# A third buffer for raw weight blocks, in place of most of the scratch for dynamic DMAs

## The chip, the cores and the metric

The kernel runs on one core of one Trainium2 chip. The metric is the time of one execution on the device in microseconds (us), lower is better. Before and after compute the same outputs from the same inputs, all in fp32; matrix products are done in three passes of a rounded type (below). Engines are named as the profile names them: PE (matmul), PEld (PE's weight load), DVE (vector), ACT (scalar), POOL (GpSimd), SP (the queue from which all DMAs here are issued).

## What is computed

Two blocks, one after the other, on 512 tokens of 1024 features (16 learned tokens are put ahead in the first). The first has a state-space mixer with 16 heads (SSD), a second mixer of 64 small diagonal recurrences (S5), and an MLP; the second is two layers of convolution, neighbourhood attention, a gated merge and a convolutional FFN, with a context stream of 256 tokens beside the main one. Cut to the part in which the change reorders most:

```python
proj = n @ w_in[layer]                 # z, xbc, dt and u, from the normed tokens
xbc = jax.nn.silu(_causal_depthwise_conv(proj[..., o_xbc:o_dt], conv_w[layer], conv_b[layer]))
y_ssd = _ssd_mixer(xbc, dt_raw, z, ...)
y_s5 = _s5_mixer(u, ...)               # recurrence over time in 64 groups, then:
#   y = gelu(y);  v = y @ w_glu + b_glu;  y = v[:, :D_S5] * sigmoid(v[:, D_S5:])
h = h + concatenate([y_ssd, y_s5]) @ w_out[layer]
h = h + square(relu(rmsnorm(h) @ w_up[layer])) @ w_down[layer]
return second_block(first_block(...), c_2, ctx_2, ...)
```

## The kernel before

**Weights.** All large weights stream from HBM once, in blocks of 128 partitions x 1024 fp32 (512 KB, 4 KB of each partition; some are narrower). The helper `W` (lines 222 to 242) fetches one: a DMA on SP into a tile `raw`, of which there are RAW buffers; ACT rounds it to the type fp32r (`whi`, line 239); DVE subtracts, so that `wlo` = raw - whi (line 241). Of `whi` and `wlo` there are HL = 3 buffers each. A raw buffer is free when its line 241 has read it.

```python
with self.tc.high_priority(offset=self.AHEAD):
    raw = self.wp.tile([P, 1024], F32, tag="raw", name=f"raw{i}", bufs=self.RAW)[:, :cols]
    nc.sync.dma_start(raw, src[:, part * cols:(part + 1) * cols])
with self.tc.high_priority(offset=self.SPLIT):
    ...
    hi = part("hi")
    nc.scalar.copy(hi, raw)
    lo = part("lo")
    nc.vector.tensor_sub(lo, raw, hi.bitcast(F32))
```

**Products.** `gemm` calls `mm3` (lines 247 to 249) for each block of 128 features: whi x high part, whi x low part, wlo x high part of the activations, three matmuls into one PSUM tile. A block of 1024 x 128 with 528 tokens is 48 matmuls of 264 columns.

**Order.** A tile framework schedules the program: it lets each engine's instructions run in an order that it chooses at build time from its own estimate of durations and from priorities, and puts the waits between them. AHEAD = 100 and SPLIT = 70 let a weight's DMA and its two roundings go ahead of work that was written before them. At run time each engine then works strictly in that order.

**The first block's mixers** (`build`, about 50 to 306 us). The letters of ORDER interleave two sorts of work. One is gemms on independent weights: `xbc_proj` (twelve, tiles `xbc`), `z_proj` (`z0` to `z3`, two weights each) and `dt_proj` (`dt`). The other is eight rounds of S5: `s5_prepare` m makes three tables (X transposed on PE at line 815, tile XT, and copied to P; Y; K from a product Kp at line 836, written into M by eight small DMAs at line 849), `s5_scan` m runs the recurrence. A scan is a chain over three engines: PE line 873 (S), ACT 875 (copy), PE 877 (Sp), DVE 878 and 879, twice; then DVE 880 (add), ACT 882 and POOL 883, DVE 885 (the scan proper), PE 888 (Zp), DVE 889 to 891, PE lines 894 and 896 (sixteen pairs of small matmuls in all, tile y5m), ACT 899, and a DMA to DRAM (900). Tables of round m+1 are made beside the scan of round m. When all eight are done, `s5_result` loads them back (DMA 906), ACT applies gelu and rounds (lines 908 and 912, tiles yt and y50h), and `glu` starts its gemms (tiles glug and glua), which need all of it. In a row of order, a tile's first digit is the round or the number of the gemm: XT7_0 is round 7, first half; z3 and dt are the last two gemms of the in-projection.

**The context stream.** Beside the main one the second block has gemms on 256 tokens (`ctx_mix`, tiles cxg, cxb, cxo, up to 1055 us), in which a weight is used for half as long.

**Memory.** The program is built with the default scratch for dynamic DMAs, 16 KB of each partition.

Of the kernel before, what the change touches and what calls it, by code (L numbers as in the profile page):

```python
# [190 lines left out]
class Builder:  # L191
    AHEAD = 100
    CONV = (600, 300)
    ADALOW, CXCONV = 0, 0
    RAW = 2
    HL = 3
    TABLES = 5
    ADA1 = 12
# [23 lines left out]
    def W(self, name, *idx, cols=1024, part=0, tags=None):  # L222
# [8 lines left out]
# [3 lines that stand above are left out]
# [1492 lines left out]


# [11 lines left out]
```

## Time and profile before

| | us |
|---|---|
| median of 3 runs | 2740.7 (2732.67 to 2740.95) |
| the profiled execution | 2738.33 |
| its span, first to last instruction | 2736.6 |
| busy PE / DVE / ACT / POOL in it | 2675.2 / 2041.1 / 1165.5 / 6.0 |
| mean granted TensorE clock | 0.995 of full |

Times inside the kernel are microseconds from the start of the span of the profiled execution. A busy PE is not one at its peak: matmuls overlap in the pipeline, so that a matmul of 264 columns has a duration of 0.28 us while the next starts 0.12 us after it. The distance between starts is therefore what a matmul costs.

### The profile page before, as it was taken

The numbers are of one execution on the slowest core, as the hardware profiler recorded it, in microseconds if no ns is written. First come the engines' busy times: TensorE is split into PE (matmuls) and PEld (weight loads), VectorE is DVE, ScalarE is ACT, GpSimd is POOL, SyncE is SP. The second block draws the span as 40 slices with busy tenths as digits, with TensorE's granted clock in tenths as the row PEclk, the third lists the DMA queues.
The fourth block names the chain that finished last, engine by engine and source line by source line (L and its number), as shares of the span: only waits on it lengthen the run. The fifth ranks groups of instructions, "written<-read, shape, count | busy, mean of one in ns | idle before, by whom it ended". The sixth has DMA issues, their size and how long they took to land.

```text
span 2736.6 us, 39800 instructions
## 1 busy us (share of the span) xinstructions
PE 2675.2 (98%) x15107; PEld 2269.9 (83%) x15107; DVE 2041.1 (75%) x3986; ACT 1165.5 (43%) x1961; POOL 6.0 (0%) x52
## 2 busy tenths in 40 slices
PE   8999899999999999999999999999999999999998
PEld 8898678788887898777788888888887777988887
DVE  7987678999885675898669888644769976655556
ACT  4443664433543553445454232322553454534333
POOL 0000000000000000000000000000000000000000
PEclk9999999999999999999999999999999999999999
DMA  6222435566332345322324446211342223232322
GB/s 210 72 82 76 120 124 169 165 205 196 124 108 96 121 148 181 97 89 85 106 85 148 149 153 217 93 61 63 106 145 92 89 66 96 92 97 87 109 93 77
DMA packets 157390, 321.02 MB, mean 117 GB/s; under 512 B 39760, under 2 KB 60688, under 8 KB 157200
## 3 DMA queue, kind: packets, MB, share of 16 engines
q1 hardware_dynamic: 157200, 318.49, 36.9%
q8 instruction: 119, 1.95, 0.3%
q14 instruction: 71, 0.58, 0.1%
HBM read 306.53 MB, written 9.54 MB: 115 GB/s over the span
## 4 chain that ended last, share of the span: by engine, by line
PE 78%; DVE 12%; DMA 4%; ACT 3%; issue 2%; SPq 0%; DVEq 0%; ACTq 0%; POOL 0%
PE lat1fu L247 3%; PE lat1fu L249 3%; PE lat1fu L248 3%; DVE wlo L241 3%; PE lat0fu L248 3%; PE lat0fu L247 3%; PE lat0fu L249 3%; PE dn L247 2%; PE dn L249 2%; PE dn L248 2%; PE up L248 2%; PE up L247 2%; PE up L249 2%; PE lat1d L248 1%; PE lat1d L247 1%
## 5 line engine op out<-in xcount | busy, mean ns | idle before, releaser
L239 ACT CAST whi<-raw 128x1024 fp32r<-128x1024 f32 (+3 forms) x486 | 456.7, 940 | 854.5 <-PE ctx0d L248 118.5
L241 DVE TENSOR_TENSOR wlo<-raw,whi 128x1024 fp32r<-128x1024 f32 (+3 forms) x486 | 526.7, 1084 | 196.2 <-ACT whi L239 190.3
L248 PE MATMUL ctx0fu<-ctx0fx,whi 128*128 128x256 f32 x352 | 99.7, 283 | 0.0
L249 PE MATMUL ctx0fu<-ctx0fx,wlo 128*128 128x256 f32 x352 | 99.6, 283 | 0.0
L247 PE MATMUL ctx0fu<-ctx0fx,whi 128*128 128x256 f32 x352 | 99.5, 283 | 0.0
L1137 DVE SCALAR_TENSOR_TENSOR lat0cv<-lat0u,vect,lat0cv 128x512 f32<-128x512 f32 x120 | 85.7, 746 | 0.5
L1137 DVE SCALAR_TENSOR_TENSOR lat1cv<-lat1u,vect,lat1cv 128x512 f32<-128x512 f32 x120 | 85.7, 744 | 0.5
L1468 DVE SCALAR_TENSOR_TENSOR lat0fc<-lat0fu,vect,lat0fc 128x511 f32<-128x511 f32 x44 | 32.9, 748 | 63.5 <-ACT lat0fc L1467 63.5
L248 PEld LDWEIGHTS ctx0fu<-ctx0fx,whi 128*128 128x128 f32 x352 | 67.4, 191 | 1.6
L247 PEld LDWEIGHTS ctx0fu<-ctx0fx,whi 128*128 128x128 f32 x352 | 67.4, 191 | 1.6
L249 PEld LDWEIGHTS ctx0fu<-ctx0fx,wlo 128*128 128x128 f32 x352 | 67.4, 191 | 0.0
L1467 ACT ACTIVATE lat0fc<-lat0fu,vect 128x512 f32<-128x512 f32 x44 | 34.3, 778 | 74.5 <-PE lat0fu L249 74.5
L1508 DVE SCALAR_TENSOR_TENSOR hT<-lat1d,mod1lat,hT 128x512 f32<-128x512 f32 (+1 forms) x40 | 25.5, 643 | 48.2 <-PE lat1d L249 48.0
L1137 DVE SCALAR_TENSOR_TENSOR cxcv<-cxu,vect,cxcv 128x256 f32<-128x256 f32 x120 | 52.6, 480 | 0.8
L249 PE MATMUL ctx0d<-ctx0fh,wlo 128*128 128x256 f32 x176 | 50.5, 288 | 0.5 <-DVE wlo L241 0.5
L248 PE MATMUL ctx0d<-ctx0fh,whi 128*128 128x256 f32 x176 | 50.4, 287 | 0.0
L247 PE MATMUL ctx0d<-ctx0fh,whi 128*128 128x256 f32 x176 | 50.0, 285 | 0.2 <-ACT whi L239 0.2
L988 DVE TENSOR_TENSOR hT<-hT,dn 128x512 f32<-128x512 f32 x40 | 27.4, 684 | 28.7 <-PE dn L249 28.7
L981 DVE SCALAR_TENSOR_TENSOR r<-up,rsbm 128x512 f32<-128x512 f32 x32 | 22.1, 690 | 31.7 <-PE up L249 31.7
L1508 DVE SCALAR_TENSOR_TENSOR hT<-lat0d,mod0lat,hT 128x512 f32<-128x512 f32 x32 | 23.9, 748 | 20.9 <-PE lat0d L249 20.9
L249 PE MATMUL cxg<-cxn1x,wlo 128*128 128x256 f32 x128 | 36.3, 284 | 0.4 <-DVE wlo L241 0.4
L247 PE MATMUL cxg<-cxn1x,whi 128*128 128x256 f32 x128 | 36.3, 284 | 0.0
(3104 smaller groups left out, 8944.2 us busy)
## 6 DMA issues: line engine op xcount, KB each, us to landing
raw<-in_p_in SPq DMA_DIRECT2D x100, 512.0 KB, 3.5
aw<-in_ada SPq DMA_DIRECT2D x192, 256.0 KB, 3.1
raw<-in_p_up SPq DMA_DIRECT2D x88, 512.0 KB, 3.5
raw<-in_p_dn SPq DMA_DIRECT2D x48, 384.0 KB, 3.0
raw<-in_w_up SPq DMA_DIRECT2D x32, 512.0 KB, 3.6
raw<-in_p_cn SPq DMA_DIRECT2D x48, 256.0 KB, 2.6
raw<-in_w_down SPq DMA_DIRECT2D x24, 384.0 KB, 3.0
raw<-in_p_out SPq DMA_DIRECT2D x18, 512.0 KB, 3.6
```

Source lines behind the costliest of these rows:

```text
L239: nc.scalar.copy(hi, raw)
L241: nc.vector.tensor_sub(lo, raw, hi.bitcast(F32))
L247: mm(ps, w[0], x[0], start=first, stop=False)
L248: mm(ps, w[0], x[1], start=False, stop=False)
L249: mm(ps, w[1], x[0], start=False, stop=last)
L981: V.scalar_tensor_tensor(r, ps, 0.0, rsb, op0=ALU.max, op1=ALU.mult)
L988: V.tensor_add(h[f], h[f], ps)
L1137: V.scalar_tensor_tensor(ac, u[:, k:k + n], self.vec(f"cdw{l}", 4 * k + i), ac, op0=ALU.mult, op1=ALU.add)
L1467: A.activation(u, ps[:, :n], AF.Identity, scale=wv(1), bias=self.vec(f"fdwb{l}", t))
L1468: V.scalar_tensor_tensor(u[:, 1:], ps[:, :n - 1], wv(0), u[:, 1:], op0=ALU.mult, op1=ALU.add)
L1508: V.scalar_tensor_tensor(x, ps, self.mod[l, kind][:, 40 + f:41 + f], x, op0=ALU.mult, op1=ALU.add)
```

## The change

RAW goes from 2 to 3, so 4 KB more of each partition hold raw blocks, and the scratch for dynamic DMAs is cut from 16 KB to 4 KB of each partition. No instruction is added or removed. The schedule is made anew with the third buffer.

```diff
-    RAW = 2
+    RAW = 3
...
-    nc = bacc.Bacc("TRN2", target_bir_lowering=False, num_devices=1)
+    nc = bacc.Bacc("TRN2", target_bir_lowering=False, num_devices=1,
+                   dynamic_dma_scratch_size=4096)
```

Of the 14,370 matmul instructions on PE, some 1,250 stand at another place in the order; 1,059 of these lie between 100 and 283 us of the trace before. Three places follow.

On PE, the start of the tables of the last S5 round (XT7) and of the scan of the one before (S6), as it stood before; dt is a gemm of the in-projection:

```order
L247 MATMUL dt_1_2973<-xg0h_103,whi26_2968 16x264
L248 MATMUL dt_1_2973<-xg0l_104,whi26_2968 16x264
L815 MATMUL XT7_0_2273<-cst_78,X7_2263 128x128 x4
L815 MATMUL XT7_1_2279<-cst_78,X7_2263 128x128 x4
L836 MATMUL Kp7_0_2295<-Y7_2285,bc7_2261 16x128 x4
L836 MATMUL Kp7_1_2301<-Y7_2285,bc7_2261 16x128 x4
L873 MATMUL S6_0_2331<-hT5_86,P6_2017 128x66 x4
L249 MATMUL dt_0_2972<-xg0h_103,wlo26_2970 16x264
L249 MATMUL dt_1_2973<-xg0h_103,wlo26_2970 16x264
L247 MATMUL dt_0_2972<-xg1h_107,whi26_2968 16x264
```

The same place in the changed kernel; z3 is the last gemm of the in-projection, and the two rows shown of it are its last two:

```order
L248 MATMUL z3_1_3065<-wlo28_3124,xg7h_131 128x256
L249 MATMUL z3_1_3065<-whi28_3122,xg7l_132 128x256
L815 MATMUL XT7_0_2273<-cst_78,X7_2263 128x128 x4
L815 MATMUL XT7_1_2279<-cst_78,X7_2263 128x128 x4
L836 MATMUL Kp7_0_2295<-Y7_2285,bc7_2261 16x128 x4
L836 MATMUL Kp7_1_2301<-Y7_2285,bc7_2261 16x128 x4
L873 MATMUL S6_0_2331<-hT5_86,P6_2017 128x66 x4
L877 MATMUL Sp6_0_2337<-S6_2330,cst_78 128x264
L873 MATMUL S6_1_2341<-hT5_86,P6_2017 128x66 x4
L877 MATMUL Sp6_1_2347<-S6_2330,cst_78 128x264
L888 MATMUL Zp6_0_2355<-S6_2330,cst_78 128x264
L888 MATMUL Zp6_1_2359<-S6_2330,cst_78 128x264
```

Before, 140 matmuls of gemms stood between XT7 and the last row of the S5 scans (44 of dt, 96 of z3); now all 140 stand ahead of XT7 and none behind it.

On PE, the first half of the scan of round 1, before:

```order
L873 MATMUL S1_0_1272<-hT2_83,P1_958 128x66 x4
L249 MATMUL xbc1_0_1644<-xg0h_103,wlo13_1642 128x264
L249 MATMUL xbc1_1_1645<-xg0h_103,wlo13_1642 128x264
L247 MATMUL xbc1_0_1644<-xg1h_107,whi13_1640 128x264
L248 MATMUL xbc1_0_1644<-xg1l_108,whi13_1640 128x264
L249 MATMUL xbc1_0_1644<-xg1h_107,wlo13_1642 128x264
L247 MATMUL xbc1_1_1645<-xg1h_107,whi13_1640 128x264
L248 MATMUL xbc1_1_1645<-xg1l_108,whi13_1640 128x264
L249 MATMUL xbc1_1_1645<-xg1h_107,wlo13_1642 128x264
L247 MATMUL xbc1_0_1644<-xg2h_111,whi13_1640 128x264
L248 MATMUL xbc1_0_1644<-xg2l_112,whi13_1640 128x264
L877 MATMUL Sp1_0_1278<-S1_1271,cst_78 128x264
```

and now:

```order
L873 MATMUL S1_0_1272<-hT2_83,P1_958 128x66 x4
L247 MATMUL xbc2_0_2135<-xg0h_103,whi16_2131 128x264
L248 MATMUL xbc2_0_2135<-xg0l_104,whi16_2131 128x264
L877 MATMUL Sp1_0_1278<-S1_1271,cst_78 128x264
L873 MATMUL S1_1_1282<-hT2_83,P1_958 128x66 x4
L247 MATMUL xbc2_1_2136<-xg0h_103,whi16_2131 128x264
L248 MATMUL xbc2_1_2136<-xg0l_104,whi16_2131 128x264
L877 MATMUL Sp1_1_1288<-S1_1271,cst_78 128x264
```

Ten gemm matmuls stood between S and Sp there, now two; in the other rounds up to the sixth they are between 2 and 18.

On DVE, the middle of the scan of round 6, before (wlo28 is the last weight of z3):

```order
L880 TENSOR_TENSOR t6_2320<-t6_2320,f6_2319 128x528
L565 SCALAR_TENSOR_TENSOR xbcT7_2960<-xr7_2956,vect_79,xbcT7_2960 128x528
L241 TENSOR_TENSOR wlo28_3124<-raw28_3120,whi28_3122 128x1024
L885 SCALAR_TENSOR_TENSOR S6_2330<-f6_2319,t6_2320 128x528
L890 TENSOR_TENSOR t6_2320<-S6_2330,cs6_2322 128x264 x2
```

and now:

```order
L880 TENSOR_TENSOR t6_2320<-t6_2320,f6_2319 128x528
L885 SCALAR_TENSOR_TENSOR S6_2330<-f6_2319,t6_2320 128x528
L890 TENSOR_TENSOR t6_2320<-S6_2330,cs6_2322 128x264 x2
L889 TENSOR_TENSOR f6_2319<-Zp6_0_2355,sn6_2321 128x264
L889 TENSOR_TENSOR f6_2319<-Zp6_1_2359,sn6_2321 128x264
```

The work of the gemms on DVE (the convolution of line 565, the residue of line 241) has moved ahead of the chain of the scan.

## Rows read from the trace of the kernel before

**Rows 1.** The page, part 1: busy time of each engine, share, instructions.

```profile
PE 2675.2 (98%) x15107; PEld 2269.9 (83%) x15107; DVE 2041.1 (75%) x3986; ACT 1165.5 (43%) x1961; POOL 6.0 (0%) x52
```

**Rows 2.** One stretch: from:to length, busy us by engine, clock, DMA share, GB/s.

```profile
246.27:282.60 36.33, 35.01 (x280) 31.72 (x278) 24.61 (x43) 16.04 (x28) 0.23 (x2) 1.00 0.31 96
```

**Rows 3.** Waits of PE from 88 to 246 us: total us, times, longest.

```profile
PE Zp L888 <- DVE S L885: 2.6, 6, 0.7
PE xbc L247 <- ACT whi L239: 2.4, 2, 1.3
PE xbc L249 <- DVE wlo L241: 1.4, 1, 1.4
```

**Rows 4.** PE in order of time, end of S5: start, us, instruction, idle before.

```profile
246.27 1.04 PE L815 MATMUL XT<-cst,X 128*128 128x128 f32 x8
...
252.09 0.61 PE L877 MATMUL Sp<-S,cst 128*128 128x264 f32 x2
...
259.61 1.13 PE L888 MATMUL Zp<-S,cst 128*128 128x264 f32 x4 [0.48 <-DVE S L885]
...
262.40 0.33 PE L896 MATMUL y<-t,Y 128*128 128x64 f32 x2
...
269.64 0.61 PE L877 MATMUL Sp<-S,cst 128*128 128x264 f32 x2
...
279.06 0.43 PE L896 MATMUL y<-t,Y 128*128 128x64 f32 x2 [0.33 <-DVE t L891]
...
282.24 0.39 PE L896 MATMUL y<-t,Y 128*128 128x64 f32 x2
...
290.59 0.80 PE L247 MATMUL glug<-y50h,whi 128*128 128x512 f32 x1 [7.61 <-ACT y50h L912]
```

**Rows 5.** DVE in order of time, the same stretch.

```profile
255.78 0.70 DVE L880 TENSOR_TENSOR t<-t,f 128x528 f32<-128x528 f32 x1
256.40 0.76 DVE L565 SCALAR_TENSOR_TENSOR xbcT<-xr,vect,xbcT 128x528 f32<-128x528 f32 x1
257.08 1.22 DVE L241 TENSOR_TENSOR wlo<-raw,whi 128x1024 fp32r<-128x1024 f32 x1
258.21 1.25 DVE L885 TENSOR_TENSOR_SCAN S<-f,t 128x528 f32<-128x528 f32 x1
...
275.70 1.20 DVE L241 TENSOR_TENSOR wlo<-raw,whi 128x1024 fp32r<-128x1024 f32 x1
```

**Rows 6.** ACT in order of time, the same stretch.

```profile
251.39 0.35 ACT L875 COPY S<-S 128x264 f32<-128x264 f32 x1
...
267.99 0.37 ACT L875 COPY S<-S 128x264 f32<-128x264 f32 x1
```

**Rows 7.** PE in order of time: two neighbours of a gemm.

```profile
124.01 0.28 PE L249 MATMUL z<-whi,xg0l 128*128 128x256 f32 x1
124.13 0.28 PE L247 MATMUL z<-whi,xg1h 128*128 128x256 f32 x1
```

**Rows 8.** PE in order of time: XT transposes, four each, at three places.

```profile
68.53 0.66 PE L815 MATMUL XT<-cst,X 128*128 128x128 f32 x4 [2.75 <-DVE X L809]
...
71.08 1.12 PE L815 MATMUL XT<-cst,X 128*128 128x128 f32 x4 [0.45 <-DVE X L809]
...
80.69 0.60 PE L815 MATMUL XT<-cst,X 128*128 128x128 f32 x4
```

**Rows 9.** The stretch of the second of these, columns as in rows 2.

```profile
69.71:73.12 3.41, 2.96 (x15) 2.65 (x14) 3.41 (x8) 2.17 (x4) 0.00 (x0) 0.50 0.18 68
```

**Rows 10.** Waits of PE from 1005 to 1052 us, columns as in rows 3.

```profile
PE cxo L249 <- DVE wlo L241: 2.6, 5, 0.8
PE cxo L247 <- ACT whi L239: 1.9, 1, 1.9
```

**Rows 11.** Waits of PE, whole span: its longest for a weight outside rows 3, 10.

```profile
PE ctx0d L249 <- DVE wlo L241: 0.5, 1, 0.5
```

**Rows 12.** The page, part 6: issues of one raw weight, count, size, us to landing.

```profile
raw<-in_p_in SPq DMA_DIRECT2D x100, 512.0 KB, 3.5
```

## The prediction

> **What bounds the kernel now.** I read the busy times first, then what PE waits for, then the stretch in which the change reorders most, engine by engine. PE is busy for 2675.2 of 2736.6 us [rows 1]: all waits of PE together hold some 61 us, and a change that removes no matmul can win at most a part of that. So the question is only at which places PE stands still, and whether the new order makes more or fewer of them. Two sorts matter here. PE waits for weights: between 88 and 246 us for whi and wlo of xbc, 2.4 + 1.4 us [rows 3], and near 1030 us for those of cxo, 2.6 + 1.9 us [rows 10]. And PE waits for S5. In the mixers' stage the gemms are cover: an S5 round is a chain over PE, ACT, DVE and a DMA in which PE has little to do, and PE fills the time with gemms. The end shows it. From XT7 at 246.27 us to the last matmul of S5 near 282.6 us PE is busy for 35.0 of 36.3 us [rows 2], because 140 gemm matmuls stand among the steps of the chain; from there to 290.59 us, when glu starts, nothing is left to do and PE waits 7.6 us in one piece [rows 4].
>
> **The change, part by part.** A raw block can be fetched, rounded and used one block earlier. The scheduler used this to put gemms ahead of S5 steps from the second round on. No work is added; what moves is the cover.
>
> *The cover of the last two scans is gone.* In the new order of PE all of dt and z3 stands ahead of XT7. A gemm matmul costs 0.12 us from start to start [rows 7], so XT7 comes 140 x 0.12 = 16.8 us later than it would. All of that counts unless the chain behind XT7 becomes shorter by as much.
>
> *The chain behind XT7.* It took 290.59 - 246.27 = 44.3 us [rows 4]. Without gemms among its steps it loses only the places where a gemm held it up. Sp of round 6 was ready when ACT's copy ended at 251.39 + 0.35 = 251.74 [rows 6] and started at 252.09 [rows 4]: 0.3. DVE did a convolution step and a residue between the add, which ended at 256.48, and the scan at 258.21 us [rows 5]; ACT and POOL write the scan's factors in the same time, so I count half of these 1.7 us, 0.9, as lost to DVE's other work. A second convolution step like it stood ahead of the add, 0.8. Together 1.7. The first L896 of round 6 stood behind six gemm matmuls, 6 x 0.12 = 0.7, of which I count 0.4 in its 2.8 us behind Zp [rows 4]. Sp of round 7 was ready at 267.99 + 0.37 = 268.36 [rows 6], started at 269.64 [rows 4]: 1.2. A residue of a glu weight held DVE at 275.70 [rows 5] ahead of the step behind Zp: 0.7. Sum 4.3 us. The rest, 40.0 us, is latency of the chain itself: copies, the scan, sixteen pairs of small matmuls, and at the end the way through DRAM and gelu, 282.6 to 290.6 us. So -4.3; between 0 and -4.3, and I take the full sum since each part has its row.
>
> *The clock.* [...] Without cover PE stands still for 3 us and more at several steps: from the second Sp of round 6, about 2 us after the first at 252.09, to Zp at 259.61 [rows 4] it now has nothing to do, even when 2.0 us are taken off for the trims above. From the first of these on the clock should be low for most of the 30 us left. On the chain then lie the y matmuls of two rounds (279.06 to 282.6 [rows 4], 3.5 us each) and S, Sp and Zp of round 7 and Zp of round 6, about 2.9 us: at most +9.9. If the busy bursts bring the clock back, nothing. I take +7.
>
> *Waits for weights in the rounds before.* From 88 to 246 us PE's waits for weights are 2.4 and 1.4 us [rows 3]. Where the one of 1.4 us stands, the order of PE and DVE has not changed, so it stays; the two that make 2.4 go, for the blocks are now rounded much earlier in ACT's order: -2.4, with smaller ones -2.8. The waits of Zp for the scan, 2.6 [rows 3], are S5's own and stay. Against it, cover is thinner at round 1: two gemm matmuls between S and Sp instead of ten, 8 x 0.12 = 1.0, and less than before also in its second half; +1.8. Together -1, between -7.2 (the waits of rows 3, and some 0.8 of smaller ones, all gone) and +6 (1.2 us in each of five rounds).
>
> *The context stream near 1030 us.* Four residues stand earlier on DVE than before, but the rounding on ACT that ends the longest wait does not move. Of 4.5 us [rows 10] and a low clock of 3.4 us that follows, I take -2; between 0 and -6.6. In the rest of the kernel a handful of rows changes place; I cost it at nothing, since PE's longest wait for a weight there is 0.5 us [rows 11], and a block used for the full 512 tokens covers the 1.2 us that DVE needs to split one [rows 5].
>
> *The scratch.* Every DMA of the program is issued on SP; a raw block lands 3.5 us after its issue [rows 12]. [...]
>
> Sum: 16.8 - 4.3 + 7 - 1 - 2 = +16.5 us. The profiled execution took 2738.3 us, 2.4 us under the median of the runs shown (2740.7): 2738.3 + 16.5 = 2754.8, so 2755 us. What a measurement of this kernel can tell from no change is about 0.3%, 8.2 us.
>
> **The rivals.** *The clock holds and the waits go:* 16.8 - 4.3 + 0 - 2.8 - 2 = +7.7, 2746 us, at the edge of what can be measured. For it: bursts of PE work of up to 4 us stand in the bare chain. Against: one wait of 2.75 us came right ahead of the fall at 69.71 us [rows 8, 9].
>
> *The buffer pays (faster):* if the end of S5 is bound by PE's queue and not by the chain, the 44.3 us shrink by the whole 16.8 us of gemms to 27.5, and only the gains stay: -2.8 - 6.6 = -9.4, 2729 us. It decides once the chain without cover takes less than some 29 us. For it speaks that PE was busy for 35.0 of 36.3 us [rows 2]. Against it, the parts above: at only five places a step of the chain stood behind a gemm's work, 4.3 us together. [...] The trace speaks against it, for little of PE's waiting is for DMAs.
>
> *The cover is missing in all rounds (slower still):* each of five rounds loses 1.2 us more at S and Sp, and the clock stays low throughout: 16.8 - 4.3 + 9.9 + 6 = +28.4, 2767 us. [...]
>
> **How the numbers follow.** Forecast (bare chain at a mostly low clock, 2748 to 2763 us): 0.64. The clock holds: 0.18. The buffer pays: 0.04. Cover missing everywhere: 0.12. The scratch: 0.02. The ends of all terms give 2738.3 + 16.8 - 4.3 - 7.2 - 6.6 = 2737 and 2738.3 + 16.8 + 9.9 + 6 = 2771; leaving out one in ten at each side I give 2743 to 2767. Faster by over 0.3%: 0.04. Within 0.3%: three quarters of the second case, 0.14. Slower: 0.82.
>
> **What would show it.** In the changed profile PE should run from 88 us to XT7 with fewer waits than before, and reach XT7 near 262 us (+16); from there to the first glu matmul PE should be busy for well under half of some 47 us, with the granted clock at 0.5 for most of it, and waits named Sp after ACT S, Zp after DVE S and y after DVE t. glu should start near 307 us; from there on everything should run as before, shifted by that. If XT7 comes at 250 us or glu by 291 us, the count of the cover is wrong; if the bare chain takes 40 us, the clock held; if a place after 310 us moves by over 5 us, I have missed a part.

## The result, and the profile after

The changed kernel takes 2755.3 us (median of 4 runs, 2752.95 to 2755.55), the kernel before 2738.9 us in the same comparison (4 runs, 2732.67 to 2740.95): a ratio of 1.0067 with a 95% interval of 1.0052 to 1.0081. It is slower by 16 us, as forecast (2755 us, range 2743 to 2767). The terms of the sum are another matter: the loss up to glu was some 9 us larger than forecast and the gain behind it some 9 us larger too, and the two errors cancel.

The profiled execution of the changed kernel took 2755.36 us, its span is 2753.2 us, its mean granted clock 0.985 (0.995 before). The first line of its page answers to [rows 1]: no work was added, yet PE is busy for 11.6 us more. While the granted clock was 0.50, neighbours of a gemm in the changed kernel started 0.22 us apart (69.85 and 70.07 us), outside such pieces 0.12 us (72.55 and 72.67 us).

```profile
PE 2686.8 (98%) x15107; PEld 2282.9 (83%) x15107; DVE 2038.7 (74%) x3986; ACT 1164.8 (42%) x1961; POOL 6.0 (0%) x52
```

The next rows are stretches of the changed kernel, columns as in [rows 2]: the S5 rounds up to XT7; the chain behind XT7; the wait ahead of glu; the piece of time in which the granted clock was 0.50 without a break; and two such pieces in the rounds.

```profile
88.00:265.00 177.00, 171.31 (x1327) 160.85 (x1326) 142.92 (x244) 68.39 (x115) 1.68 (x15) 0.97 0.27 77
265.00:310.90 45.90, 31.67 (x138) 27.41 (x136) 19.74 (x37) 10.96 (x21) 0.23 (x2) 0.56 0.20 66
310.90:318.50 7.60, 0.63 (x6) 0.51 (x5) 0.50 (x4) 4.10 (x6) 0.00 (x0) 0.50 1.04 219
270.36:321.56 51.20, 31.43 (x116) 26.96 (x117) 19.76 (x37) 12.94 (x21) 0.23 (x2) 0.50 0.36 82
...
92.86:99.69 6.83, 6.54 (x26) 6.13 (x27) 4.13 (x8) 1.35 (x3) 0.00 (x0) 0.50 0.19 48
127.00:130.41 3.41, 3.41 (x14) 2.93 (x14) 2.72 (x6) 0.64 (x2) 0.00 (x0) 0.50 0.33 50
```

And PE in order of time behind XT7, to be laid beside [rows 4]:

```profile
265.00 1.04 PE L815 MATMUL XT<-cst,X 128*128 128x128 f32 x8
...
271.73 1.25 PE L877 MATMUL Sp<-S,cst 128*128 128x264 f32 x2 [2.81 <-ACT S L875]
...
275.06 1.25 PE L877 MATMUL Sp<-S,cst 128*128 128x264 f32 x2 [0.47 <-ACT S L875]
279.84 2.10 PE L888 MATMUL Zp<-S,cst 128*128 128x264 f32 x4 [3.54 <-DVE S L885]
...
283.76 0.63 PE L896 MATMUL y<-t,Y 128*128 128x64 f32 x2
...
292.91 1.25 PE L877 MATMUL Sp<-S,cst 128*128 128x264 f32 x2 [2.55 <-ACT S L875]
...
300.92 2.12 PE L888 MATMUL Zp<-S,cst 128*128 128x264 f32 x4 [3.45 <-DVE S L885]
...
304.32 0.69 PE L896 MATMUL y<-t,Y 128*128 128x64 f32 x2 [0.95 <-DVE t L891]
...
310.35 0.64 PE L896 MATMUL y<-t,Y 128*128 128x64 f32 x2
...
318.52 0.80 PE L247 MATMUL glug<-y50h,whi 128*128 128x512 f32 x1 [6.99 <-ACT y50h L912]
```

Read against [rows 4], this is the whole story in three distances. XT7 starts at 265.00 instead of 246.27 us: +18.7 (forecast: near 262, +16). From XT7 to glu pass 53.5 us instead of 44.3: +9.2 (forecast +2.7, some 47 us). And glu starts 27.9 us late, but the last reduction of the program (the last row of PE) is only 17.0 us late: behind glu 11.0 us are won back (forecast: 2).

### The profile page after: what moved, and what is told of

The parts are those of the page before. It is cut to its first block, busy times and chain, and to the rows that moved or that the text cites. A ratio compares the mean times of both kernels' runs of the same rounds, so it can differ in the third digit from the quotient of the medians.

```text
span 2753.2 us, 39854 instructions
## 1 busy us (share of the span) xinstructions
PE 2686.8 (98%) x15107; PEld 2282.9 (83%) x15107; DVE 2038.7 (74%) x3986; ACT 1164.8 (42%) x1961; POOL 6.0 (0%) x52
## 4 chain that ended last, share of the span: by engine, by line
PE 84%; DVE 10%; ACT 2%; DMA 2%; issue 2%; SPq 0%; DVEq 0%; POOL 0%; ACTq 0%
PE lat1fu L247 3%; PE lat1fu L248 3%; PE lat1fu L249 3%; PE lat0fu L247 3%; PE lat0fu L248 3%; PE lat0fu L249 3%; PE dn L247 2%; PE dn L249 2%; PE dn L248 2%; PE up L248 2%; PE up L249 2%; PE up L247 2%; DVE wlo L241 2%; PE lat0d L248 1%; PE lat0d L249 1%
## 5 line engine op out<-in xcount | busy, mean ns | idle before, releaser
L247 PE MATMUL cxg<-cxn1x,whi 128*128 128x256 f32 x128 | 36.3, 284 | 0.0
L248 PE MATMUL cxg<-cxn1x,whi 128*128 128x256 f32 x128 | 36.3, 284 | 0.0
```

The costliest lines, as they stand in the source:

```text
L247: mm(ps, w[0], x[0], start=first, stop=False)
L248: mm(ps, w[0], x[1], start=False, stop=False)
```

## The experiments

Each kernel was run beside the kernel before on the same chip (2739.2 to 2740.0 us there). XT7 and glu stand for the starts of these rows on PE, and a shift is that against the profiled execution of before. Single executions of one order differ too: `scratch_only` below, with the order of before, takes 45.1 us from XT7 to glu where before took 44.3, and 4.4 us more from glu to the last row of PE.

### The scratch alone

```diff
-    RAW = 3
+    RAW = 2
```

(against the changed kernel: two raw buffers, the small scratch; every engine's order is that of before)

> Two raw buffers as before, the scratch for dynamic DMAs at 4 KB as after: only the memory part of the change. The order on every engine is that of before. Theory (the time lies in the new order): same as before within 0.3%, 2735 to 2743 us. Rival (the smaller scratch slows DMAs): slower, up to after's 2755 us, with raw blocks landing later than 3.5 us after issue.

Measured: 2741.3 us, ratio 1.0004 [0.9995 to 1.0013]. The scratch costs nothing that can be seen. All that follows is the third buffer.

### The third buffer in one half of the program

`two_then_three` has two raw buffers until the first block's mixers are done and three from there on; `three_then_two` the other way round (the diff is that of the first).

```diff
-            raw = self.wp.tile([P, 1024], F32, tag="raw", name=f"raw{i}", bufs=self.RAW)[:, :cols]
+            raw = self.wp.tile([P, 1024], F32, tag=self.RT[0], name=f"raw{i}", bufs=self.RT[1])[:, :cols]
...
             self.SM = 16
+            self.RT = ("rawb", 3)
```

> Two raw buffers up to the end of the first block's mixers, then three others (a tag of their own): the second half of the change alone. Up to 510 us the order is nearly that of before. Theory (the loss is the lost cover of the last two S5 scans, +28 us at glu, and the rest of the kernel gives 11 us back): faster than before by 11 us, about 2728 us, glu at 290 to 292 us. Rival (the gains behind 1000 us in after are a matter of the shifted clock and not of the buffer): 2737 to 2740 us. Rival (a third buffer costs something everywhere): slower than before.

> Three raw buffers up to the end of the first block's mixers, two others after it: the first half of the change alone. Theory: the whole loss and no gain, 2739 + 28 = about 2767 us, glu at 318 us as in after. Rival (the first half costs less than the trace of one execution says): 2750 us or less.

Measured: `two_then_three` 2729.4 us, ratio 0.9958 [0.9945 to 0.9972]; `three_then_two` 2769.0 us, ratio 1.0105 [1.0091 to 1.0119]. The signs separate: in the mixers the third buffer costs (glu 24.9 us late in the profile of `three_then_two`, and 25.3 at the end, so nothing comes back), behind them it gains (in `two_then_three` glu is 2.2 us late, the end 6.4 us early: 8.6 us within one profiled execution, 10 by the medians). The change as made is the sum of a loss and a gain; the medians of the two halves, +29.5 and -10.1 us, add up to 3 us more than its +16.4.

### Extra matmuls in the bare chain: what the clock costs

Before, with gemms among the steps of the chain, the clock was 1.00 there [rows 2]. If the low clock is what makes the chain 53.5 us long, other work in the place of the gemms may hold it up and shorten the chain. The first try put extra matmuls, whose results are not read, into unused columns of the Sp tiles of rounds 6 and 7.

```diff
+    def cover(self, m, n, pp, x):
+        for _ in range(n if m >= 6 else 0):
+            self.nc.tensor.matmul(pp[:, HALF:512], self.C("perm"), x[:, :512 - HALF],
+                                  start=True, stop=True)
...
             pp = self.mps(f"Sp{m}_{q}")
+            if q == 0:
+                self.cover(m, 5, pp, self.yp if m == 7 else self.pm7)
             T.matmul(pp[:, :HALF], self.C("perm"), S[:, hf[q]], start=True, stop=True)
+            self.cover(m, 10 if q else 1, pp, S[:, hf[q]])
```

> The changed kernel with 32 extra matmuls whose results nobody reads, in the PE waits of the last two S5 scans: five between S and the first Sp, one behind it, ten behind the second Sp, in rounds 6 and 7. They take the place of the lost cover as far as PE's activity goes and do none of its work. [...] Rival (the chain is as long at full clock, since it waits for ACT and DVE): clock at 1.0, XT7 to glu still over 50 us, 2753 to 2757 us. Rival (the extra matmuls delay the chain themselves): slower than after.

Measured: 2763.8 us, ratio 1.0088 [1.0074 to 1.0101], slower than the changed kernel: the second rival. PE in order of time shows why the run says little of the clock:

```profile
274.17 4.35 PE L855 MATMUL Sp<-S,cst 128*128 128x248 f32 x20
...
282.05 1.13 PE L897 MATMUL Zp<-S,cst 128*128 128x264 f32 x4 [3.54 <-DVE S L894]
```

The ten extra matmuls (20 rows) write the tile that DVE's next step reads, so that step waits for them, and Zp still waits 3.5 us for the scan. XT7 to glu takes 59.7 us, and the clock falls all the same (mean 0.81 from 265.0 to 310.9 us): it is 0.50 from 283.38 us on for 13.7 us and once more from 307.27 us on. The second try gives them PSUM tiles of their own:

```diff
+    def cover(self, m, n, x, q):
+        if m >= 6:
+            pd = self.mps(f"dm{m}_{q}")
+            for _ in range(n):
+                self.nc.tensor.matmul(pd[:, :248], self.C("perm"), x[:, :248],
+                                      start=True, stop=True)
...
+            if q == 0:
+                self.cover(m, 2 if m == 7 else 5, self.yp if m == 7 else self.pm7, q)
             pp = self.mps(f"Sp{m}_{q}")
             T.matmul(pp[:, :HALF], self.C("perm"), S[:, hf[q]], start=True, stop=True)
+            if q:
+                self.cover(m, 9, S[:, hf[q]], q)
```

> The changed kernel with extra matmuls of 248 columns, whose results nobody reads, in the bare chain: five behind S6_0, nine behind Sp6_1, two behind S7_0 and nine behind Sp7_1, each row of them in a PSUM tile of its own, so that no step of the chain waits for them except on PE itself. Theory (the low clock makes the bare chain 10 us or so longer than it was with gemms among its steps): the granted clock stays at full speed for most of the stretch behind XT7, the y matmuls of a round take about 3.5 us instead of 6.6, XT7 to glu takes 41 to 46 us instead of 53.5, and the time is 2745 to 2750 us, 6 to 10 under the changed kernel. Rival (the chain is as long at full clock, since it is waiting and not matmuls): XT7 to glu stays at 51 to 55 us, the time at 2753 to 2757 us. Second rival (too little activity to hold the clock): the clock falls all the same, time 2754 to 2760 us.

Measured: 2747.4 us, ratio 1.0032 [1.0020 to 1.0044]: 8 us less than the changed kernel, with more work on PE. One stretch from XT7 to glu, and three rows of PE and DVE of this kernel:

```profile
261.28:306.52 45.24, 30.47 (x194) 26.05 (x192) 20.18 (x41) 15.24 (x27) 0.23 (x2) 0.93 0.39 104
```

```profile
274.89 1.26 DVE L897 TENSOR_TENSOR_SCAN S<-f,t 128x528 f32<-128x528 f32 x1 [2.66 <-PE dm L857]
276.21 1.16 PE L900 MATMUL Zp<-S,cst 128*128 128x264 f32 x4 [1.42 <-DVE S L897]
...
306.52 0.80 PE L247 MATMUL glug<-y50h,whi 128*128 128x512 f32 x1 [7.52 <-ACT y50h L925]
```

XT7 to glu is 45.2 us instead of 53.5. From XT7 on the clock stayed at 1.00 until 299.88 us, behind the last y matmul (mean 0.93 to glu, the first row). DVE, ACT, POOL and the DMA queue work in the order of the changed kernel here. So at least 8.3 us of the chain were the clock's, for even so the extra matmuls still hold up the chain: they read the tile S that the scan (line 897 here) writes, and the scan is idle for 2.66 us where it is idle for 0.92 in the changed kernel. (In this profiled execution XT7 also comes 3.7 us earlier than in the changed kernel's, through its start and the clock in the rounds; the extra matmuls stand behind that.) A third try lets them read the round's input instead:

```diff
-                self.cover(m, 2 if m == 7 else 5, self.yp if m == 7 else self.pm7, q)
+                self.cover(m, 2 if m == 7 else 5, U, q)
...
-                self.cover(m, 9, S[:, hf[q]], q)
+                self.cover(m, 8, U, q)
```

> The changed kernel with extra matmuls in the bare chain as in the run chain_covered_apart (results not read), but eight instead of nine behind each second Sp, and all of them read the input U of the round, which no step writes. There the extra matmuls read the scan's tile S, and DVE's scan, which writes S, waited for the last of them: its idle time was 2.66 us in each of the two rounds, against 0.92 us for the scans in the changed kernel. Theory: the chain is shorter by some 2 x 1.7 us, XT7 to glu takes 41 to 43 us instead of 45.2 (the bare chain at full clock, forecast at 40.0), time 2742 to 2746 us. Rival (the two waits are not on the path, or the clock falls again since less runs): XT7 to glu 45 us or more, time 2747 us or more.

Measured: 2748.0 us, ratio 1.0036 [1.0023 to 1.0050]; XT7 to glu 45.6 us. The expectation of 41 to 43 us failed, and the rival's numbers hold, by its second reading (the clock falls again). In round 6 the hold-up is gone as expected (Zp 13.1 us behind XT7, not 14.9), but in round 7 the two extra matmuls behind S, which read the input now and wait for nothing, run early, PE stands still for 2.55 us ahead of Sp, and the granted clock is 0.50 from 282.93 us on for 6.8 us. It falls again at 296.58 us, ahead of the last y matmuls of the round (298.79). The rows are DVE's and PE's:

```profile
273.20 1.26 DVE L897 TENSOR_TENSOR_SCAN S<-f,t 128x528 f32<-128x528 f32 x1 [0.92 <-POOL f L895]
```

```profile
274.52 1.16 PE L900 MATMUL Zp<-S,cst 128*128 128x264 f32 x4
...
283.47 1.25 PE L887 MATMUL Sp<-S,cst 128*128 128x264 f32 x2 [2.55 <-ACT S L883]
```

The two runs together give the chain at full clock, piece by piece. The first three pieces are from the third try, the last two from the second, less the 2.66 - 0.92 = 1.74 us of its second scan; the sum is an estimate, for no single run has all five.

| piece | before | changed | at full clock |
|---|---|---|---|
| XT7 to the first Sp of round 6 | 5.82 | 6.73 | 6.90 |
| to Zp of round 6 | 7.52 | 8.11 | 6.18 |
| to its first y matmul on t | 2.79 | 3.92 | 2.94 |
| to Zp of round 7 | 13.44 | 17.16 | 12.29 |
| to glu | 14.75 | 17.60 | 13.86 |
| sum | 44.3 | 53.5 | 42.2 |

### The third buffer throughout, with the old cover

If order is all, three buffers with the cover put back must lose nothing in the mixers. Here a weight's DMA is held back by a copy of one column, which waits for X of a named round.

```diff
+    GATE = {18: 4, 19: 4, 20: 4, 21: 5, 22: 5, 23: 6, 24: 6, 25: 6, 26: 7, 27: 7, 28: 7}
...
+            m = self.GATE.get(i)
+            if m is not None:
+                nc.vector.tensor_copy(raw[:, :1], self.gt[:, m:m + 1])
             nc.sync.dma_start(raw, src[:, part * cols:(part + 1) * cols])
...
+        if m >= 4:
+            V.tensor_copy(self.gt[:, m:m + 1], X[:, 1023:1024])
```

> The changed kernel, three raw buffers and the small scratch throughout, with the DMAs of the weights 18 to 28 held back until X of a named S5 round is written (18 to 20: round 4; 21 and 22: round 5; 23 to 25: round 6; 26 to 28: round 7), by a copy of one column on DVE for each. So the last gemms of the in-projection stand behind XT7 again, 145 gemm matmuls, as 140 did in the kernel before, and the last 91 of them ahead of glu. Theory (all the loss is that the third buffer let the cover run ahead): XT7 near 247 to 252 us, glu at 288 to 296 us, the gains behind 310 us stay at 8 to 11 us, time 2725 to 2735 us. Rival (the third buffer itself costs in the first part, by DMAs or by roundings that get in the way of S5): glu stays near 310 us or later, time 2745 us or more.

Measured: 2753.0 us, ratio 1.0049 [1.0036 to 1.0063]; XT7 10.3 us late, glu 22.6 us late. The theory's time failed. The gates put 288 gemm matmuls between XT7 and glu, not the 145 that the expectation names; 143 of them stand behind the last y matmul, and from there to glu pass 17.9 us, 8.2 before. And the place of the loss moved with the cover: held back to round 4, no weight is ready there, and no gemm matmul stands from XT4 to the second Sp of round 3. Between XT4 and XT5 this kernel loses 16.6 us (7.5 us of shift, though 76 gemm matmuls, 9.1 us, fewer run there), and from 166.88 us on, just ahead of XT4 (170.29), the granted clock is 0.50 for 23.9 us. That stretch, then a wait of PE from 60 to 330 us (us, times, longest):

```profile
166.88:190.77 23.89, 20.22 (x83) 16.39 (x82) 16.78 (x33) 7.63 (x14) 0.21 (x2) 0.50 0.23 57
```

```profile
PE XT L822 <- DVE X L814: 8.2, 5, 4.6
```

So a finer gate, chosen so that the counts of the kernel before are met within 9 matmuls in every round:

```diff
-    GATE = {18: 4, 19: 4, 20: 4, 21: 5, 22: 5, 23: 6, 24: 6, 25: 6, 26: 7, 27: 7, 28: 7}
+    GATE = {13: 1, 14: 1, 15: 1, 16: 2, 17: 2, 18: 2, 19: 3, 20: 3, 21: 4, 22: 4, 23: 4,
+            24: 5, 25: 5, 26: 6, 27: 6, 28: 7}
...
-        if m >= 4:
+        if m >= 1:
             V.tensor_copy(self.gt[:, m:m + 1], X[:, 1023:1024])
```

> Three raw buffers and the small scratch throughout, with the DMAs of the weights 13 to 28 each held back until X of a named S5 round is written, the rounds chosen so that the gemm matmuls behind XT2 to XT7 and ahead of glu are within 15 of those of the kernel before in every round (140 behind XT7). Theory (what the third buffer loses in the first block is its order alone: where the cover stands): XT7 within 4 us of the kernel before, glu at 288 to 296 us, the gains behind 310 us stay, time 2725 to 2735 us. Rival (another block in flight costs by itself, through DMAs or roundings at the wrong time): glu at 300 us or later, time 2740 us or more.

Measured: 2737.1 us, ratio 0.9993 [0.9984 to 1.0002], so 18 us of the changed kernel's time are back with three buffers all through; XT7 is 6.5 us late, glu 8.0. Both numbers miss what the theory asked for (4 us; 296 us or earlier), by a loss in one place: XT2 is already 4.4 us late, and from XT2 to glu only 3.7 us are added, where the changed kernel adds 21.9 (from 6.1 to 27.9). DVE and then PE at that place:

```profile
109.57 2.38 DVE L570 SCALAR_TENSOR_TENSOR xbcT<-xr,vect,xbcT 128x528 f32<-128x528 f32 x3 [2.96 <-ACT xbcT L567]
```

```profile
114.41 1.11 PE L822 MATMUL XT<-cst,X 128*128 128x128 f32 x4 [6.22 <-DVE X L814]
```

Convolution steps stand ahead of X of round 2 on DVE, wait there for ACT, and PE waits for X; the granted clock is 0.50 there from 110.02 us on for 10.2 us. Read so, that is again the order that the scheduler chose and not a block in flight; it was argued from these rows, and no run took these steps away. Neither the time nor glu came out as the rival has them (2740 us; 300 us or later), and what is left of it behind XT2 would be under the 3.7 us.

### A fourth buffer behind the mixers

```diff
-    RAW = 3
+    RAW = 2
...
+                    tc.tile_pool(name="rp", bufs=1) as self.rp, \
...
+                    tc.tile_pool(name="rp2", bufs=1) as self.rp, \
...
+                self.RAW = 4
```

(two buffers until the mixers are done, four from there on, each set in a pool of its own)

> The small scratch, two raw buffers until the mixers of the first block are done, four from there on. Theory (each further buffer removes waits for weights behind 310 us): two then three buffers took 10.1 us off the kernel before; a fourth buffer takes away at most what is left of PE's waits for weights there, 0 to 4 us: time 2725 to 2730 us. Rival (what the third buffer gained came from the order and not from the number, so a fourth moves it at random): 2728 to 2740 us.

Measured: 2733.1 us, ratio 0.9981 [0.9972 to 0.9990]: faster than before, 4 us slower than `two_then_three`, a time inside the rival's range. One wait is new, at the start of the first block's MLP, where the second pool opens and no weight could be fetched ahead (waits of PE from 420 to 530 us; there were 1.6 us here, for activations):

```profile
PE up L247 <- ACT whi L239: 5.5, 1, 5.5
```

This wait comes with the second pool and not with the fourth buffer: the MLP's first weight is issued at 515.7 us here, in `two_then_three`, whose three buffers lie in the old pool, at 511.4. From the first matmul of the context stream to the last row of PE this kernel takes 1819.3 us, `two_then_three` 1818.0, the kernel before 1828.3. So behind the wait the fourth buffer brings no more than the third, which the theory allows (0 to 4 us); that order and not number decides, the rival's reason, is not shown by this run.

## Why the prediction was right, and where its steps were not

| term, us | forecast | measured |
|---|---|---|
| cover behind XT7 gone | +16.8 | +16.8 |
| waits in the rounds before | -1 | -0.8 |
| low clock in the rounds | not seen | +2.8 |
| chain, trims | -4.3 | -2.1 (estimate, table above) |
| chain, low clock | +7 | +11.3 (53.5 - 42.2) |
| scratch | 0 | 0 (ratio 1.0004) |
| behind glu | -2 | -11.0 |
| sum | +16.5 | +17.0 |

Apart from the scratch, the measured terms are differences of profiled executions; in all, 2755.36 - 2738.33 = 17.0 us. The 0 for the scratch, and its chance of 0.02, were the author's assumption, which no row of the kernel before shows; `scratch_only` measured a ratio of 1.0004 [0.9995 to 1.0013].

**The cover** is right. No gemm matmul stands behind XT7, and the runs that put gemms (`weights_pinned_finer`) or other matmuls (`chain_covered_apart`) back there recover time.

**The waits in the rounds.** PE was idle for 158.27 - 150.93 = 7.3 us from 88 us to XT7 before (the same stretch, below), 177.00 - 171.31 = 5.7 us after. So idle time fell by 1.7, and the two waits for whi in [rows 3] are gone as forecast, while the one of 1.4 us for wlo stays; one of 1.1 us for DVE's xr is new. Part of the 1.7 is only that PE itself was slower, as the next paragraph shows; -0.8 is what is left with the clock at full speed.

```profile
88.00:246.27 158.27, 150.93 (x1187) 141.94 (x1187) 138.29 (x236) 63.15 (x108) 1.59 (x15) 1.00 0.28 79
```

**The clock in the rounds** was missed. In the same two rows PE is busy for 20.4 us more. The 140 more matmuls (1327 against 1187) cost 16.8 us of that; 3.6 us are left, and for 10.2 us of these rounds the granted clock was 0.50 (the two pieces above), which it was nowhere in this stretch before. Two runs with PE's order of the changed kernel up to XT7 show what that is worth, for in their profiled executions the clock did not fall in the rounds. The stretch from the same row near 88 us to XT7, in `chain_covered_free` and then in `three_then_two`:

```profile
87.18:261.44 174.26, 167.55 (x1327) 156.90 (x1327) 142.79 (x244) 68.47 (x115) 1.68 (x15) 1.00 0.28 78
87.47:261.75 174.28, 167.60 (x1327) 156.95 (x1327) 142.78 (x244) 68.41 (x115) 1.68 (x15) 1.00 0.28 78
```

The changed kernel takes 177.1 us from that row (87.93 to 265.00), so the low clock cost 2.8 us there, and not every execution pays it. At full clock the rounds take 16.0 us more than before (174.3 against 158.3), 16.8 - 0.8: nearly the forecast of 16.8 - 1. The prediction put a price on thinner cover as waits (+1.8) and a low clock behind XT7 alone.

**The chain's trims** were half of the forecast. Where a gemm's residue and convolution left DVE, from Sp to Zp of round 6, 1.3 us of the forecast 1.7 came. Most of the loss is ahead of it: XT7 to the first Sp should have become shorter by 0.3 and became longer by 0.9 to 1.1. The 0.3 came, for Sp now starts 0.05 us behind the end of ACT's copy, but the copy ends 1.2 us later behind XT7. ACT's rows name the step that the prediction didn't look at; before, the first copy of P started 0.64 us behind XT7 (first row), in the changed kernel 1.86 us (the others):

```profile
246.91 0.59 ACT L816 COPY P<-XT 128x512 f32<-128x512 f32 x1 [2.35 <-PE XT L815]
```

```profile
265.20 0.84 ACT L592 ACTIVATE z<-z,rs1k 128x256 f32<-128x256 f32 x2 [1.98 <-PE z L249]
265.93 1.04 ACT L239 CAST whi<-raw 128x1024 fp32r<-128x1024 f32 x1
266.86 0.59 ACT L816 COPY P<-XT 128x512 f32<-128x512 f32 x1
...
269.72 0.64 ACT L784 ACTIVATE cs<-f 128x528 f32<-128x528 f32 x1
...
271.33 0.35 ACT L875 COPY S<-S 128x264 f32<-128x264 f32 x1
```

The rounding of a glu weight (line 239; no other gemm's weight is left then) and the last step of z3 now stand ahead of P on ACT. ACT has no idle time from 265.20 us to the copy that Sp waits for, and from P to that copy it takes 4.5 us in both kernels. The prediction moved weights past instructions of PE and DVE, and did not cost their roundings ahead of the chain's steps on ACT. That this rounding, moved away, would bring the 1 us back was argued from these rows and was not tried. Another step looks like the cause and is not: DVE waits 2.57 us for the small DMA of dI, issued on SP behind three glu weights.

```profile
268.63 0.28 DVE L843 TENSOR_TENSOR dI<-dI,cst 16x128 f32<-16x128 f32 x1 [2.57 <-DMA dI<-in_d]
268.84 0.69 DVE L783 TENSOR_TENSOR f<-f,t 128x528 f32<-128x528 f32 x1
```

ACT's line 784 needs line 783, which ended at 269.53 us. But ACT was busy with its copies until it started line 784 at 269.72, without a gap, so the chain lost nothing by the wait here.

**The chain's clock** was mis-sized, +7 against +11.3, above the bound of 9.9. No run shows the +7 as a term: it was the author's estimate, with the steps of the chain on PE taken as twice as long for most of 30 us, where [rows 8, 9] show it for four transposes in 3.41 us only (1.12 us, 0.60 to 0.66 outside); in its place the runs show the 11.3. The bound counted Zp of round 6 and what follows; the clock fell at 270.36 us already, so S and the second Sp of round 6 ran slow as well (3.33 us from the first Sp to the second, 2.02 in `chain_covered_free`). The y matmuls did nearly as forecast: 6.0 us from the first to the last L896 row of a round (304.32 to 310.35), 3.2 before (279.06 to 282.24 [rows 4]), so 2.9 more where the bound had 3.5. The prediction's "glu should start near 307 us" is a slip beside this: it takes off the 2 us of the context stream, which lies behind glu; its terms up to glu add up to +18.5, so 309 us. Measured are 318.5.

**Behind glu** the prediction looked at the context stream near 1030 us and costed the rest at nothing, since no wait for a weight there is longer than 0.5 us [rows 11]. The context stream gave 2.4 us (the shift against before falls from 27.8 us at its start, 901 us, to 25.4 at 1103 us): its waits for wlo shrank from 2.6 [rows 10] to 0.5, that for whi grew from 1.9 to 3.2.

```profile
PE cxo L247 <- ACT whi L239: 3.2, 1, 3.2
...
PE cxo L249 <- DVE wlo L241: 0.5, 1, 0.5
```

Half of the 11.0, 5.4 us, came between 1664 and 1996 us of before, a place whose longest waits are for activations; the last 2.9 us came behind that. The prediction's own sign for a missed part (a place after 310 us that moves by over 5 us) is met. The two halves of this stretch, before and then after (from the same row of PE to the same row, so the lengths can be compared), and two waits of PE that were there before and have no row after (the first at 1668.55 us, the second at 2342.96 us, in the part behind the stretch):

```profile
1663.86:1935.75 271.89, 270.42 (x1547) 238.65 (x1546) 153.34 (x266) 78.34 (x119) 0.46 (x6) 0.99 0.29 94
1935.75:1996.38 60.63, 59.22 (x395) 53.65 (x394) 52.66 (x110) 38.20 (x70) 0.00 (x0) 1.00 0.47 144
```

```profile
1689.19:1958.40 269.21, 268.86 (x1547) 237.23 (x1546) 151.22 (x263) 78.32 (x119) 0.45 (x6) 1.00 0.29 94
1958.40:2016.28 57.88, 57.70 (x395) 53.30 (x394) 53.47 (x112) 39.68 (x73) 0.00 (x0) 1.00 0.51 159
```

```profile
PE lat0d L247 <- ACT lat0fh11h L298: 1.1, 1, 1.1
...
PE lat1fass L366 <- DVE lat1fasq L357: 1.0, 1, 1.0
```

The two take 332.5 us before and 327.1 after, 5.4 less: idle time of PE fell from 2.9 to 0.5 us, and its busy time from 329.6 to 326.6. So 2.4 of the 5.4 stood among the waits, in pieces of at most 1.1 us. The granted clock was 0.50 for 3.4 us behind one of them, near 1670 us; `three_then_two`, with two buffers and the clock at 1.00 in the same stretch, is busy for 328.0 us, so some 1.6 of the 3.1 us of busy time are the clock's. The other 1.4 have no row: PE's rows overlap, a matmul lasts 0.28 us and the next starts 0.12 us after it [rows 7], so a hold-up of up to 0.16 us between two matmuls is inside busy time. The step that failed is the reading "no wait for a weight over 0.5 us, so nothing to win": it left out waits for activations, the clock behind them and what the overlap hides. Why the order with three buffers has fewer of them there was not traced step by step; `two_then_three` shows that they come from the third buffer behind the mixers (8.6 us in its profile), `two_then_four` that they don't grow with the number (328.5 us in this stretch, 326.6 in `two_then_three`). The gain is no accident of one execution: from glu to the last row of PE the three profiled executions with two buffers there (before, `scratch_only`, `three_then_two`) take 2438.7 to 2443.1 us, the seven with three 2427.7 to 2432.9.

**The rivals.** "The clock holds" is out by the 51 us at 0.50. "The cover is missing in all rounds" was partly true (2.8 us were lost in the rounds, by the clock and not by the waits at S and Sp that it names, and the chain's clock went over its bound) and would alone have given some 2766 us; the gain behind glu hid it, and `three_then_two`, which has that gain taken away, is at 2769 us. "The buffer pays" is false of the change as made. In the part of the program where no scan needs cover the buffer does pay: there `two_then_three` measured 10 us of gain. So a right total here is owed to two errors of some 9 us each that cancel; the range of 2743 to 2767 was honest about the size of the terms, but not about the gain behind glu, which outside the context stream had no bound at all in the sum.

## What to carry to other kernels

A deeper prefetch changes what an automatic scheduler puts first, so count, place by place, how much independent work is left beside each latency chain in the new order: here the loss was 140 matmuls of cover (16.8 us), and it grew by two thirds (11.3 us, an estimate) because the clock fell in the bare chain. Where one half of a program gains from a buffer and another loses, give it to the half that gains: two buffers in the mixers and three behind them are the fastest version found, 2729.4 us, 0.9958 of the kernel before. And when weights are moved earlier, look at every engine on which they are worked on: here one rounding of a weight on ACT came to stand ahead of a chain's step and cost the chain some 1 us. A wait that a row shows, like DVE's 2.57 us for a small load, costs only if nothing else holds up the step behind it.

## What the runs showed of the hardware

The granted clock fell to 0.50 at 270.36 us, during PE's wait of 2.81 us ahead of Sp (271.73 us), and then stayed there in one piece for 51.2 us, through two rounds in which PE was busy for 31.4 us, and until 3 us into glu's gemms. Before, the same rounds with gemms among the steps ran at 1.00 [rows 2]. With extra matmuls among the steps it was 1.00 from XT7 to 299.88 us in `chain_covered_apart`, and that kernel took 2747.4 us, 8 us less than the changed kernel. In `chain_covered_free` PE waited 2.55 us ahead of Sp of round 7, with extra matmuls before and behind it, and the clock was 0.50 for 6.8 us from that wait on. A wait of PE ahead of the transposes XT of round 0 was 2.75 us long in the kernel before and 1.99 us in the changed kernel, and the clock was 0.50 for 3.4 us from 69.71 and 68.97 us on. The length of a wait alone did not decide it: two waits of the kernel before, of 1.93 and 1.92 us, differ in what followed. Behind the first the clock was 0.50 for 3.4 us from 1028.86 us on, behind the second it stayed at 1.00. The rows are PE's, then the stretches behind the two waits:

```profile
1027.82 0.39 PE L247 MATMUL cxo<-cxm,whi 128*128 128x256 f32 x1 [1.93 <-ACT whi L239]
...
1167.28 0.63 PE L1212 MATMUL lat_0s<-cst,lat_0p 128*128 128x128 f32 x4 [1.92 <-DVE lat_0p L1210]
```

```profile
1028.86:1032.27 3.41, 3.19 (x15) 3.19 (x16) 3.12 (x7) 3.41 (x7) 0.00 (x0) 0.50 0.49 183
1167.28:1185.00 17.72, 17.72 (x101) 12.40 (x102) 15.58 (x43) 8.96 (x21) 0.00 (x0) 1.00 0.16 53
```
